# Two projections of a mixing block, moved in 512 columns of half the depth instead of 256 columns of the whole depth

## The chip, the cores and the metric

The kernel runs on one core of a Trainium2 chip. The metric is the device time of one execution in microseconds (us). A core has a matrix engine (TensorE, PE in the profile), a vector engine (VectorE, DVE), an activation engine (ScalarE, ACT), GpSimd (POOL) and SyncE (SP), which here issues the weight transfers. Matrix products are made in 128x128 steps: a stationary tile is loaded, a moving tile of up to 512 columns streams past it, and the sum stands in one of eight PSUM banks, 512 float32 columns wide.

## The reference

A first block of two layers works on x (512 tokens, width 1024, float32); each layer has a gated feed-forward part, a mix part and a second feed-forward part. A second block follows, which the change doesn't touch. The mix part is this:

```python
u = rmsnorm(x, g_mix[l])
p = u @ w_in[l]                       # width 3712: Fourier 1024, dilated 3 x 384, differential q, k, v 3 x 512
a_in = p[..., :c0]                    # Fourier
qc, kc, vc = p[..., c3:c4], p[..., c4:c5], p[..., c5:]
y_a = fourier_mix(a_in) @ w_br_a[l]   # real part of a 2-D DFT over tokens and the 128 channels of each of 8 groups
y_b = dilated_mixture(qb, kb, vb, rel_bias[:, :DIL_HEADS]) @ w_br_b[l]
y_c = diff_attention(qc, kc, vc, ...) @ w_br_c[l]
gates = jax.nn.sigmoid(u @ w_gate[l] + b_gate[l]).reshape(Bsz, S, N_BRANCHES, D)
merged = gates[:, :, 0] * y_a + gates[:, :, 1] * y_b + gates[:, :, 2] * y_c
x = x + merged @ w_out[l]
```

The two projections that change are `a_in` (1024 columns) and `vc` (512 columns), each 512 tokens by 1024 deep.

## The kernel before

x is held transposed, as 8 tiles of 128 channels x 512 tokens. Every float32 operand is split into a high part and a low part (`hi`, `lo`), and `mm3` (lines 196 to 199) makes each product of three matmuls: high x high (L197), high x low (L198), low x high (L199). Two kinds of projection are made so. `form_a` leaves the result transposed: the weights are stationary and 512 tokens move. `form_b` leaves tokens in the partitions: 128 tokens of x are stationary and the weights move. `form_b_pair` (L503) runs `form_b` for two token tiles into the two halves of one PSUM bank, 256 weight columns each, and evicts each half with ACT.

`weights` (L98) brings a chunk of weights, usually 128 x 8 x 256 (8 depth tiles of 256 columns): one DMA issued by SyncE into `raw` (tag `wr`), then two pieces, each a copy by ACT into `wh` (L108) and a subtraction by DVE into `wl` (L109). The tags `wr`, `wh` and `wl` have two buffers each, so two split chunks can exist, and a third one's split waits until every matmul of the first has run. Work tiles of 128 x 512 have the tag `g`, of which there are 32.

`mix` writes the work of a layer in one order: the dilated and differential q and k projections, the values projection (two chunks of 256 columns, between steps of the dilated attention), the differential attention interleaved with the gates of branches 1 and 2 (18 rounds; rounds 16 and 17 hold `project(0)` and `project(1)`), then the Fourier branch interleaved with its gates. The Fourier branch has four chunks of 256 columns, two groups each. `project(c)` makes the projection, adds and subtracts the token halves and splits these into parts; `sequence(c)` transforms over the tokens from the parts; `channels(c)` transforms over the channels and leaves tiles for the last merge.

The framework (Tile) derives all waits and orders each engine's queue with a planner: it takes the first written instruction that is ready by its own reckoning of time. So an engine's queue can leave the written order, and is fixed before the program runs; on the chip each engine takes its queue in that order.

Of the kernel before, what the change touches and what calls it, by code (L numbers as in the profile page):

```python
# [17 lines left out]
P = 128  # L18
# [32 lines left out]
class Kern:  # L51
# [45 lines left out]
    def weights(self, src, k0=0, nk=None):  # L97

        nc = self.nc
        src = src[:, k0:k0 + nk, :] if nk is not None else src  # L100
        _, nk, n = src.shape
        raw = self.wp.tile([P, nk, n], F32, tag="wr", name=self.nm("wr"), bufs=2)
        nc.sync.dma_start(raw, src)
        hi = self.wp.tile([P, nk, n], F32R, tag="wh", name=self.nm("wh"))
        lo = self.wp.tile([P, nk, n], F32R, tag="wl", name=self.nm("wl"))
        for j in range(0, n, P):
            js = slice(j, j + P)
            nc.scalar.activation(hi[:, :, js], raw[:, :, js], AF.Copy)  # L108
            nc.vector.tensor_tensor(out=lo[:, :, js], in0=raw[:, :, js], in1=hi.bitcast(F32)[:, :, js],  # L109
                                    op=ALU.subtract)  # L110
        return hi, lo
# [119 lines left out]
    def form_b(self, out, w, t, xs, start=True):  # L231

        ts = slice(t * P, (t + 1) * P)
        for k, x in enumerate(xs):
            self.mm3(out, (x[0][:, ts], x[1][:, ts]), (w[0][:, k, :], w[1][:, k, :]), start and k == 0,
                     k == len(xs) - 1)


    def tt(self, out, a, b, op, eng=None):
# [453 lines left out]
    def fourier_steps(self, l, xs, rcol, ya):  # L693
        st = {}

        def project(c):
            w = self.weights(self.ins["w_in_a"][l][c])
            a = [self.g(), self.g()]
            for t in range(0, 4, 2):
                self.form_b_pair(w, t, xs, rcol, lambda i: a[t // 2][:, i * 256:(i + 1) * 256])  # L700
            parts = []
            for op in (ALU.add, ALU.subtract):
                s = self.g()
                self.tt(s, a[0], a[1], op)
                parts.append(self.split(s))
            st[c] = parts

        def sequence(c):
            sh, sl = self.ft_seq
            parts, out = st[c], []  # L710
            for gi in range(2):
                pe, po = self.bank(), self.bank()
                for par, b in ((0, pe), (1, po)):
                    for k in range(2):
                        cs = slice(k * 256 + gi * P, k * 256 + gi * P + P)
                        at = slice(par * 256, par * 256 + 256)
                        self.mm3(b[:, 0:256], (parts[par][0][:, cs], parts[par][1][:, cs]),
                                 (sh[k][:, at], sl[k][:, at]), k == 0, k == 1)

                hi, lo = self.g(F32R), self.g(F32R)  # L720
                for b, at, ds in ((pe, 0, slice(0, 129)), (po, 0, slice(129, 385)), (pe, 129, slice(385, 512))):
                    src = b[:, at:at + ds.stop - ds.start]
                    self.split(src, hi[:, ds], lo[:, ds])
                out.append((hi, lo))
            st[c] = out

        def channels(c):
            ch, cl = self.ft_ch
            for hi, lo in st[c]:
                bu, bv = self.bank(), self.bank()  # L730
                for b, at, n, cs in ((bu, 0, 258, slice(0, P)), (bv, 256, 256, slice(P, 2 * P))):
                    self.mm3(b[:, 0:n], (ch[:, cs], cl[:, cs]), (hi[:, at:at + n], lo[:, at:at + n]), True, True)
                u, y = self.g(), self.g()
                self.act(u[:, 0:257], bu[:, 0:257], AF.Copy)
                self.act(y[:, 0:257:256], bu[:, 0:129:128], AF.Copy)
                ve, vo = bv[:, 129:256], bv[:, 1:129]
                self.tt(y[:, 2:256:2], u[:, 1:128], ve, ALU.subtract)
                self.tt(y[:, 1:256:2], u[:, 129:257], vo, ALU.subtract)
                self.tt(y[:, 510:256:-2], u[:, 1:128], ve, ALU.add)
                self.tt(y[:, 511:256:-2], u[:, 129:257], vo, ALU.add)  # L740
                ya.append(self.split(y))

        return project, sequence, channels


    def mix(self, l):
# [8 lines left out]
        def chunk(key, src):  # L755
            if key not in held:
                held.clear()
                held[key] = self.weights(src)
            return held[key]

        def dil(n):
            w = chunk(("d", n // 2), w_in[6 + n // 2] if n < 8 else ins["w_in_vb"][l])
            return self.form_a(w, n % 2, xs)

        def diff(n):
# [5 lines left out]
        def gate(i, n):  # L771
            w = chunk(("g", i, n // 2), ins["w_gate"][l][i * 4 + n // 2])
            b = self.form_a(w, n % 2, xs)
            t = self.side(n) if i == 1 else self.g()
            self.tt(t, b, R, ALU.mult)
            at = l * 24 + i * 8 + n
            self.act(t, t, AF.Tanh, scale=0.5, bias=self.bh[:, at:at + 1])
            th[i, n] = t
# [45 lines left out]
        for i in range(9):  # L824
            if i < 8:
                scores(*todo[i])
            if i > 0:
                turn(*todo[i - 1])
            if i < 7:
                diff(i + 1)  # L830
            elif i == 7:
                v = [t[:, at:at + S] for t in (self.big(), self.big()) for at in (0, S)]
                w = chunk(("v", 0), w_in[4])
                self.form_b_pair(w, 0, xs, rcol, lambda i: v[i][:, 0:256])
            else:
                self.form_b_pair(w, 2, xs, rcol, lambda i: v[2 + i][:, 0:256])
            if i > 0:
                values(*todo[i - 1])
            if i == 6:
                qk[0] = self.stacked(cT[4], cT[0])  # L840
        w = chunk(("v", 1), w_in[5])
        self.form_b_pair(w, 0, xs, rcol, lambda i: v[i][:, 256:512])
        fin()
        branch_b()
        self.form_b_pair(w, 2, xs, rcol, lambda i: v[2 + i][:, 256:512])
        scores, turn, values, finish = self.diff_steps(l, qk, v, yc)
        todo = [(h, qb) for h in range(4) for qb in range(4)]
        project, sequence, channels = self.fourier_steps(l, xs, rcol, ya)
# [28 lines left out]
        channels(0)  # L877
        project(2)
        sequence(1)
        gate(0, 2)  # L880
        channels(1)
        project(3)
        sequence(2)
        gate(0, 3)
        channels(2)
# [904 lines left out]
def layout(inputs):  # L1790
    f = {k: np.asarray(v) for k, v in inputs.items()}
    d = {"x": np.ascontiguousarray(f["x"][0].T.reshape(KD, P, S))}
    p = []
    for name, n in PARAMS:
        v = f[name]
        if name in ("s5_lambda_re_2", "s5_lambda_im_2"):
            v = v[0].reshape(16, P)
        elif name == "s5_log_dt_2":
            v = np.repeat(v[0], 64).reshape(16, P)
        p.append(_cols(v))  # L1800
    d["params"] = np.ascontiguousarray(np.concatenate(p, axis=1))
    for name in ("w_ffn1_gate", "w_ffn1_up", "w_ffn1_down", "w_ffn2_gate", "w_ffn2_up", "w_ffn2_down", "w_gate",
                 "w_br_a", "w_br_c", "w_out"):
        d[name] = _chunks(f[name])
    d["w_br_b"] = _chunks(f["w_br_b"], 512)
    w = f["w_in"]
    d["w_in_a"] = _chunks(w[:, :, 0:1024])
    order = np.concatenate([w[:, :, 2688:3200], w[:, :, 2176:2688], w[:, :, 3200:3712], w[:, :, 1024:2048]], axis=2)
    d["w_in"] = _chunks(order)
    d["w_in_vb"] = _chunks(w[:, :, 2048:2176], P)[:, 0]  # L1810
    d["rel_bias"] = f["rel_bias"]
    lam = np.stack([f["lam_q1"], f["lam_k1"], f["lam_q2"], f["lam_k2"]], axis=1)
    d["lam_v"] = lam.reshape(1, 512)
    d["even_w_in"] = _chunks(f["even_w_in_2"][0])
    d["even_w_out"] = _chunks(f["even_w_out_2"][0])
    d["s5_w_glu"] = _chunks(f["s5_w_glu_2"][0])
    w = f["odd_w_in_2"][0]
    d["odd_w_in"] = _chunks(w[:, 0:3072])
    d["odd_w_r"] = _chunks(w[:, 3072:3088], 16)[0]
    d["odd_w_out"] = _chunks(f["odd_w_out_2"][0])  # L1820
    d["gla_w_gate"] = f["gla_w_gate_2"][0]
    for n in ("s5_b_re", "s5_b_im"):
        b = f[n + "_2"][0].reshape(16, P, 16)
        d[n] = np.ascontiguousarray(b.transpose(1, 0, 2).reshape(P, 256))
    for n in ("s5_c_re", "s5_c_im"):
        c = f[n + "_2"][0].transpose(0, 2, 1).reshape(16, P, 16)
        d[n] = np.ascontiguousarray(c.transpose(1, 0, 2).reshape(P, 256))
    d.update(_consts())
    return d
# [16 lines left out]
```

## Time and profile before

| | |
|---|---|
| median of three executions | 3039.03 us (3038.86 to 3041.94) |
| profiled execution | 3038.39 us |
| its span, first to last instruction | 3036.7 us |
| PE busy | 3015.5 us, 99% |
| weight loads of PE | 2645.0 us, 87% |
| DVE busy | 2037.7 us, 67% |
| ACT busy | 1352.4 us, 45% |
| granted clock of PE | 1.00 |

The profile is of one execution; its times count from the first instruction, and the span is a little shorter than the time of the execution. A busy share is a mean over all stages. Matmuls are pipelined: the durations shown overlap, and a matmul's place in the stream is read from its start. The mix part of the first layer runs from about 339 to 830 us, that of the second from about 1533 to 2030 us. A row of the timeline has the start, the duration, engine, line, operation, tiles (out<-in by the program's names) and shape; in brackets stands the idle time of the engine before it and what ended it.

### The profile page before, as it was taken

Reading aid. Unit: us, or ns where it says so; the run is one execution under the profiler, and the core shown is the slowest. Engines: PE = TensorE matmul, PEld = TensorE weight load, DVE = VectorE, ACT = ScalarE, POOL = GpSimd, SP = SyncE. Lnnn points to the kernel's source line nnn. Section 1 sums busy time; section 2 is a strip of 40 time slices with the busy share of each in tenths; the row PEclk is TensorE's granted clock in tenths of the full one; section 3 lists DMA queues with packets and bytes.
Section 4 is the critical chain, followed back from the end, with each engine's and each line's share of the span. In section 5 each row is a group of like instructions: output and inputs, shape, how many; then the busy total and the mean of one; then the engine's idle time right before and its main releaser. Section 6 shows DMA issues by size and latency. Waiting matters only on the chain.

```text
span 3036.7 us, 44149 instructions
## 1 busy us (share of the span) xinstructions
PE 3015.5 (99%) x17718; PEld 2645.0 (87%) x17718; DVE 2037.7 (67%) x3646; ACT 1352.4 (45%) x2380; POOL 177.8 (6%) x310
## 2 busy tenths in 40 slices
PE   9999999999999999999999999999999999999999
PEld 7898889889889988889988889888999898877887
DVE  7798745646567979878874565557788855554633
ACT  5343435544343435433433554444334456663532
POOL 1001000000000011001120000000000011110010
PEclk9999999999999999999999999999999999999999
DMA  4232333322222333223343432222232332312221
GB/s 153 105 103 105 118 108 115 111 78 98 92 90 98 114 121 121 98 98 110 107 140 108 122 108 91 75 97 91 104 112 89 124 131 100 108 53 84 95 70 56
DMA packets 73358, 311.14 MB, mean 102 GB/s; under 512 B 18836, under 2 KB 20564, under 8 KB 44608
## 3 DMA queue, kind: packets, MB, share of 16 engines
q1 hardware_dynamic: 59680, 282.39, 27.0%
q10 hardware_dynamic: 9296, 16.47, 1.9%
q0 software_dynamic: 4176, 9.46, 1.2%
q8 instruction: 139, 2.28, 0.3%
q14 instruction: 67, 0.55, 0.1%
HBM read 292.47 MB, written 12.66 MB: 100 GB/s over the span
## 4 chain that ended last, share of the span: by engine, by line
PE 94%; ACT 2%; issue 1%; DVE 1%; DMA 1%; POOL 0%; SPq 0%; POOLq 0%; ACTq 0%; DVEq 0%
PE b L197 29%; PE b L199 29%; PE b L198 29%; PE b L202 7%; PE b L266 2%; ACT g L250 1%; ACT L250 0%; ACT sb L250 0%; DMA g<-tb 0%; DVE wl L109 0%; POOL sb L1259 0%; POOL y L240 0%; DVE g L240 0%; DMA g<-s_kst 0%; DMA wr<-in_w_ffn_gate 0%
## 5 line engine op out<-in xcount | busy, mean ns | idle before, releaser
L197 PE MATMUL b<-xh,wh 128*128 128x512 f32 (+1 forms) x1880 | 692.6, 368 | 7.3 <-ACT xh L250 6.8
L198 PE MATMUL b<-xl,wh 128*128 128x512 f32 (+1 forms) x1880 | 682.4, 363 | 1.1 <-DVE xl L94 1.1
L199 PE MATMUL b<-xh,wl 128*128 128x512 f32 (+1 forms) x1880 | 682.8, 363 | 0.5 <-DVE wl L94 0.5
L108 ACT ACTIVATE wh<-wr 128x1024 fp32r<-128x1024 f32 (+2 forms) x396 | 383.2, 1005 | 537.2 <-PE b L198 350.3
L109 DVE TENSOR_TENSOR wl<-wr,wh 128x1024 fp32r<-128x1024 f32 (+2 forms) x396 | 453.2, 1162 | 137.0 <-ACT wh L108 135.4
L197 PE MATMUL b<-g,wh 128*128 128x512 f32 x1168 | 456.6, 391 | 0.5 <-ACT g L93 0.5
L199 PE MATMUL b<-g,wl 128*128 128x512 f32 x1168 | 454.8, 389 | 1.2 <-DVE wl L109 1.2
L198 PE MATMUL b<-g,wh 128*128 128x512 f32 x1168 | 454.8, 389 | 0.2 <-DVE g L94 0.2
L197 PEld LDWEIGHTS b<-xh,wh 128*128 128x128 f32 x1880 | 355.7, 189 | 62.4 <-ACT xh L250 6.8
L198 PEld LDWEIGHTS b<-xl,wh 128*128 128x128 f32 x1880 | 355.8, 189 | 57.3 <-issue 2.2
L199 PEld LDWEIGHTS b<-xh,wl 128*128 128x128 f32 x1880 | 355.2, 189 | 57.8 <-DVE wl L94 0.9
L240 DVE TENSOR_TENSOR g<-b,g 128x512 f32<-128x512 f32 (+2 forms) x265 | 184.2, 699 | 235.3 <-PE b L199 220.8
L199 PEld LDWEIGHTS b<-g,wl 128*128 128x128 f32 x1168 | 219.2, 188 | 47.9 <-DVE wl L109 2.0
L197 PEld LDWEIGHTS b<-g,wh 128*128 128x128 f32 x1168 | 219.3, 188 | 47.5 <-issue 2.0
L198 PEld LDWEIGHTS b<-g,wh 128*128 128x128 f32 x1168 | 219.3, 188 | 45.3 <-DVE g L94 0.5
L197 PE MATMUL b<-wh,xh 128*128 128x256 f32 x896 | 256.9, 287 | 0.0
L198 PE MATMUL b<-wl,xh 128*128 128x256 f32 x896 | 254.5, 284 | 1.0 <-DVE wl L109 1.0
L199 PE MATMUL b<-wh,xl 128*128 128x256 f32 x896 | 253.6, 283 | 0.0
L240 DVE TENSOR_TENSOR g<-g,g 128x512 f32<-128x512 f32 (+8 forms) x371 | 200.8, 570 | 66.7 <-ACT g L250 62.3
L240 DVE TENSOR_TENSOR g<-g,b 128x256 f32<-128x256 f32 (+1 forms) x484 | 176.9, 397 | 31.2 <-PE b L199 27.3
L93 ACT ACTIVATE sw<-s 128x512 fp32r<-128x512 f32 x180 | 111.8, 630 | 193.3 <-DVE s L240 159.2
L250 ACT ACTIVATE g<-g 128x512 f32<-128x512 f32 (+4 forms) x280 | 143.6, 528 | 96.5 <-DVE g L240 88.3
(242 smaller groups left out, 5117.2 us busy)
## 6 DMA issues: line engine op xcount, KB each, us to landing
wr<-in_w_ffn_up SPq DMA_DIRECT2D x44, 1024.0 KB, 4.8
wr<-in_w_ffn_gate SPq DMA_DIRECT2D x43, 1024.0 KB, 4.8
wr<-in_w_ffn_down SPq DMA_DIRECT2D x32, 1024.0 KB, 4.8
wr<-in_w_gate SPq DMA_DIRECT2D x24, 1024.0 KB, 4.8
wr<-in_w_in SPq DMA_DIRECT2D x20, 1024.0 KB, 4.8
wr<-in_even_w_in SPq DMA_DIRECT2D x20, 1024.0 KB, 5.1
wr<-in_w_ffn_down SPq DMA_DIRECT2D x16, 768.0 KB, 4.3
g<-tb ACTq DMA_DIRECT2D x48, 256.0 KB, 3.1
```

The source lines that it names most:

```text
L93: self.nc.scalar.activation(hi, src, AF.Copy)
L108: nc.scalar.activation(hi[:, :, js], raw[:, :, js], AF.Copy)
L109: nc.vector.tensor_tensor(out=lo[:, :, js], in0=raw[:, :, js], in1=hi.bitcast(F32)[:, :, js], op=ALU.subtract)
L197: t.matmul(out, l[0], r[0], start=start, stop=False)
L198: t.matmul(out, l[0], r[1], start=False, stop=False)
L199: t.matmul(out, l[1], r[0], start=False, stop=stop)
L202: self.nc.tensor.matmul(out, l, r, start=start, stop=stop)
L240: return (eng or self.nc.vector).tensor_tensor(out=out, in0=a, in1=b, op=op)
L250: self.nc.scalar.activation(out, a, f, **kw)
L266: self.nc.tensor.transpose(out, a, self.ident)
```

## The change

Weights of the Fourier and the values projection are laid out on the host in chunks of 512 columns instead of 256 (the values get an array of their own, `w_in_v`, and the index of the dilated chunks moves by two). A new function `broad` loads such a chunk as two halves of the depth, 128 x 4 x 512 each, which have the size of a chunk before. It gives two steps. The first makes token tiles 0 and 1, one after the other, each over both halves; the second makes tiles 2 and 3, both over the first half and then both over the second. A tile fills a whole PSUM bank and is evicted by one ACT instruction of 512 columns. Two old chunks of Fourier are one pair now: `project(c)` with even c is the first step, with odd c the second, and the sums, differences and parts of both chunks are made after the second. The values projection's steps stand where its first chunk's two pairs stood, and its second chunk's two pairs, which stood around `fin()` and `branch_b()`, are gone. In the written order `gate(0, 2)` moves from before `channels(1)` and `project(3)` to behind them, and `channels(1)` to behind `project(3)`.

```diff
@@ weights
-        for j in range(0, n, P):
-            js = slice(j, j + P)
+        step = P if n < S else 256
+        for j in range(0, n, step):
+            js = slice(j, j + step)
             nc.scalar.activation(hi[:, :, js], raw[:, :, js], AF.Copy)
...
+    def broad(self, src, xs, rcol, out):
+        h = KD // 2
+        w = []
+        def step(second):
+            if not w:
+                w.extend([self.weights(src, 0, h), self.weights(src, h, h)])
+            ts = [2, 3] if second else [0, 1]
+            b = {t: self.bank() for t in ts}
+            order = [(t, i) for i in range(2) for t in ts] if second else [(t, i) for t in ts for i in range(2)]
+            for t, i in order:
+                cs = slice(t * P, (t + 1) * P)
+                for k in range(h):
+                    x = xs[i * h + k]
+                    self.mm3(b[t], (x[0][:, cs], x[1][:, cs]), (w[i][0][:, k, :], w[i][1][:, k, :]), i + k == 0,
+                             i == 1 and k == h - 1)
+                if i == 1:
+                    self.act(out(t), b[t], AF.Copy, scale=rcol[:, t:t + 1])
+        return lambda: step(False), lambda: step(True)
...
@@ fourier_steps
         def project(c):
-            w = self.weights(self.ins["w_in_a"][l][c])
-            a = [self.g(), self.g()]
-            for t in range(0, 4, 2):
-                self.form_b_pair(w, t, xs, rcol, lambda i: a[t // 2][:, i * 256:(i + 1) * 256])
-            parts = []
+            if c % 2 == 0:
+                a = st["a"] = [self.g() for _ in range(4)]
+                st["steps"] = self.broad(self.ins["w_in_a"][l][c // 2], xs, rcol, lambda t: a[t])
+                st["steps"][0]()
+                return
+            st["steps"][1]()
+            a, parts = st["a"], []
             for op in (ALU.add, ALU.subtract):
-                s = self.g()
-                self.tt(s, a[0], a[1], op)
-                parts.append(self.split(s))
-            st[c] = parts
+                parts.append([])
+                for t in range(2):
+                    s = self.g()
+                    self.tt(s, a[t], a[t + 2], op)
+                    parts[-1].append(self.split(s))
+            st[c - 1] = st[c] = parts
...
@@ mix
             elif i == 7:
                 v = [t[:, at:at + S] for t in (self.big(), self.big()) for at in (0, S)]
-                w = chunk(("v", 0), w_in[4])
-                self.form_b_pair(w, 0, xs, rcol, lambda i: v[i][:, 0:256])
+                v_steps = self.broad(ins["w_in_v"][l], xs, rcol, lambda t: v[t])
+                v_steps[0]()
             else:
-                self.form_b_pair(w, 2, xs, rcol, lambda i: v[2 + i][:, 0:256])
+                v_steps[1]()
...
-        w = chunk(("v", 1), w_in[5])
-        self.form_b_pair(w, 0, xs, rcol, lambda i: v[i][:, 256:512])
         fin()
         branch_b()
-        self.form_b_pair(w, 2, xs, rcol, lambda i: v[2 + i][:, 256:512])
...
         channels(0)
         project(2)
         sequence(1)
+        project(3)
+        channels(1)
         gate(0, 2)
-        channels(1)
-        project(3)
         sequence(2)
```

## Rows read from the trace of the kernel before

**Rows 1.** The page, part 1: busy us, share of the span, instructions.
```profile
PE 3015.5 (99%) x17718; PEld 2645.0 (87%) x17718; DVE 2037.7 (67%) x3646; ACT 1352.4 (45%) x2380; POOL 177.8 (6%) x310
```
**Rows 2.** The page, part 4: the chain that ended last, by engine.
```profile
PE 94%; ACT 2%; issue 1%; DVE 1%; DMA 1%; POOL 0%; SPq 0%; POOLq 0%; ACTq 0%; DVEq 0%
```
**Rows 3.** Windows of the mix stages: length, busy PE, PEld, DVE, ACT, POOL; clock.
```profile
339.00:830.00 491.00, 490.58 (x2704) 426.16 (x2704) 278.75 (x531) 217.65 (x431) 11.23 (x13) 1.00 0.31 104
1533.00:2030.00 497.00, 496.46 (x2746) 430.69 (x2745) 288.41 (x547) 220.98 (x438) 21.36 (x29) 1.00 0.32 106
```
**Rows 4.** Timeline of PE in project(0): start us, duration, line, operation.
```profile
632.08 0.28 PE L199 MATMUL b<-wh,xl 128*128 128x256 f32 x1
...
632.44 0.28 PE L199 MATMUL b<-wh,xl 128*128 128x256 f32 x1
```
**Rows 5.** Timeline of PE in the merge of branch 2.
```profile
671.36 0.39 PE L197 MATMUL b<-g,wh 128*128 128x512 f32 x1
...
672.04 0.39 PE L197 MATMUL b<-g,wh 128*128 128x512 f32 x1
```
**Rows 6.** PE windows in turn: project(0), merge 2, channels(0), gate(0,0), half a values chunk.
```profile
631.75:643.33 11.58, 11.58 (x99) 1.00 0.32 104
...
671.35:693.10 21.75, 21.75 (x97) 1.00 0.37 125
693.11:694.55 1.44, 1.44 (x13) 1.00 0.90 336
...
659.95:665.42 5.47, 5.47 (x26) 1.00 0.31 96
476.09:481.92 5.83, 5.83 (x51) 1.00 0.78 225
```
**Rows 7.** Timeline of ACT behind project(0): two 256-column evictions, one of 512.
```profile
643.55 0.84 ACT L250 ACTIVATE g<-b,y 128x256 f32<-128x256 f32 x2 [4.92 <-PE b L199]
...
648.72 0.59 ACT L250 ACTIVATE g<-b 128x512 f32<-128x512 f32 x1
```
**Rows 8.** DMA issues: transfers, count, KB each, median us to landing.
```profile
wr<-in_w_in_a SPq DMA_DIRECT2D x8, 1024.0 KB, 4.8
```
**Rows 9.** Timeline of DVE, second piece of the second values chunk.
```profile
476.57 1.23 DVE L109 TENSOR_TENSOR wl<-wr,wh 128x1024 fp32r<-128x1024 f32 x1 [0.20 <-ACT wh L108]
```
**Rows 10.** Timeline of ACT, both pieces of project(1)'s chunk.
```profile
630.49 1.06 ACT L108 ACTIVATE wh<-wr 128x1024 fp32r<-128x1024 f32 x1 [1.18 <-PE b L198]
...
633.82 1.04 ACT L108 ACTIVATE wh<-wr 128x1024 fp32r<-128x1024 f32 x1
```
**Rows 11.** Timeline of DVE, second piece of the same chunk.
```profile
634.90 1.23 DVE L109 TENSOR_TENSOR wl<-wr,wh 128x1024 fp32r<-128x1024 f32 x1 [0.70 <-ACT wh L108]
```
**Rows 12.** Timeline of DVE, second piece of the chunk split behind merge 2.
```profile
697.96 1.22 DVE L109 TENSOR_TENSOR wl<-wr,wh 128x1024 fp32r<-128x1024 f32 x1
```
**Rows 13.** Timeline of PE behind project(1): the values matmuls of the last round.
```profile
656.20 1.06 PE L202 MATMUL b<-sb,g 128*128 128x128 f32 x8
```
**Rows 14.** Timeline of DVE behind project(0): first sum, last part.
```profile
644.42 0.69 DVE L240 TENSOR_TENSOR g<-g,g 128x512 f32<-128x512 f32 x1 [6.76 <-ACT g L250]
...
648.85 0.68 DVE L94 TENSOR_TENSOR g<-g,g 128x512 fp32r<-128x512 f32 x1
```
**Rows 15.** Timeline of ACT, first piece of project(0)'s chunk.
```profile
613.92 1.06 ACT L108 ACTIVATE wh<-wr 128x1024 fp32r<-128x1024 f32 x1 [0.31 <-PE b L198]
```
**Rows 16.** Timeline of PE in the second block: transposes (L266), a projection (L197).
```profile
2561.04 0.48 PE L266 MATMUL b<-cc,g 128*128 128x128 f32 x2 [1.43 <-DVE g L244]
2561.28 0.37 PE L197 MATMUL b<-wh,xh 128*128 128x256 f32 x1
2561.48 0.29 PE L266 MATMUL b<-cc,g 128*128 128x128 f32 x1
```
**Rows 17.** Timeline of PE in the second block: second matmul of a projection.
```profile
2858.22 0.39 PE L198 MATMUL b<-wl,xh 128*128 128x256 f32 x1 [1.05 <-DVE wl L109]
```
**Rows 18.** Timeline of PE in round 15: the transposes ahead of a gate.
```profile
624.52 0.66 PE L266 MATMUL b<-cc,g 128*128 128x128 f32 x4 [0.42 <-DVE y L499]
```

More of the change, by code (lines that the diff above doesn't have):

```diff
@@ L714, in sequence @@
                     for k in range(2):
-                        cs = slice(k * 256 + gi * P, k * 256 + gi * P + P)
+                        cs = slice((c % 2) * 256 + gi * P, (c % 2) * 256 + gi * P + P)
                         at = slice(par * 256, par * 256 + 256)
-                        self.mm3(b[:, 0:256], (parts[par][0][:, cs], parts[par][1][:, cs]),
+                        self.mm3(b[:, 0:256], (parts[par][k][0][:, cs], parts[par][k][1][:, cs]),
                                  (sh[k][:, at], sl[k][:, at]), k == 0, k == 1)
@@ L761, in dil @@
         def dil(n):
-            w = chunk(("d", n // 2), w_in[6 + n // 2] if n < 8 else ins["w_in_vb"][l])
+            w = chunk(("d", n // 2), w_in[4 + n // 2] if n < 8 else ins["w_in_vb"][l])
             return self.form_a(w, n % 2, xs)
@@ L1806, in layout @@
     w = f["w_in"]
-    d["w_in_a"] = _chunks(w[:, :, 0:1024])
-    order = np.concatenate([w[:, :, 2688:3200], w[:, :, 2176:2688], w[:, :, 3200:3712], w[:, :, 1024:2048]], axis=2)
+    d["w_in_a"] = _chunks(w[:, :, 0:1024], 512)
+    d["w_in_v"] = _chunks(w[:, :, 3200:3712], 512)[:, 0]
+    order = np.concatenate([w[:, :, 2688:3200], w[:, :, 2176:2688], w[:, :, 1024:2048]], axis=2)
     d["w_in"] = _chunks(order)
```

## The prediction

> **What bounds the kernel now.** I read the page's first part, then its chain, then the windows by stage, then the timelines. The page has TensorE (PE) busy for 3015.5 of 3036.7 us; VectorE (DVE) stands at 67% and ScalarE (ACT) at 45% [rows 1]. The chain that ended last is PE for 94% of its length, and no other engine has over 2% [rows 2]. The change lies in the two mix stages. There PE is idle for 0.42 us of 491 and 0.54 us of 497, at a granted clock of 1.00, which is the 2.4 GHz level [rows 3]. So there is no wait to win back: only fewer or cheaper matmuls can shorten the stage, and every new PE wait is paid in full. DVE has 43% of these stages free and ACT 56% [rows 3], enough for moved work, if it comes in time.
>
> **Change 1: the matmuls.** A projection (Fourier or values) multiplies 4 token tiles by 8 depth tiles in 3 terms, 96 matmuls for 256 output columns. Per layer there are 4 such chunks for Fourier and 2 for values: 576 matmuls of 256 columns, 1152 in both layers. Afterwards half as many, 576, move 512 columns each; products and weight bytes are the same. PE's busy time can't price this, since a matmul shown with 0.28 us starts 0.12 us after the one before; starts must be read. Three steps of 256 columns take 0.36 us [rows 4], three of 512 take 0.68 us [rows 5]: 0.120 and 0.227 us each, so two halves cost 0.013 us more than one whole. Whole stretches (their counts also hold matmuls that end in them) say the same: 96 matmuls of 256 take 11.58 us and 48 take 5.83, while 96 of 512 take 21.75 [rows 6]. Before: per layer 4 x 11.58 + 4 x 5.83 = 69.6 us, for two layers 139.3. After: 3 pairs of chunks per layer at 21.75, six in all, 130.5. The saving is 8.8 us by stretches and 1152 x 0.120 - 576 x 0.227 = 7.5 by starts. The stretches of 256 columns begin behind transposes and hold the slow start of a step, which the stretch of 512 doesn't, so I take 7.8, near the lower.
>
> The Trainium skill ("TensorE: Matmul & The Clock Gate", Back-to-back issue gap) speaks against the change: it gives columns / 2.4 plus only some 2.5 ns, so 109.2 and 215.8 ns, and the sum would be 1.4 us saved. This trace has 120 and 227 ns, so the measurement decides.
>
> **Change 2: evictions, adds, splits.** Four 512-column evictions replace eight of 256 per pair of chunks. Two of 256 take 0.84 us together, one of 512 takes 0.59 [rows 7]; ACT saves about 1 us per pair, hidden, as ACT is not the bound. Adds, subtractions and part splits keep their number and shape (four 512-wide adds, four splits per pair). The pieces of the weight split keep 1024 elements (4 x 256 instead of 8 x 128). Each half is 1024 KB in 8 KB lines as before, 4.8 us to landing [rows 8], issued by SyncE as soon as one of two raw buffers is free. Cost on the path: none, while PE has other work.
>
> **Change 3: both weight buffers are held at once.** This is the risk. A pair needs both halves, and there are two buffers. The second half can be split only when the preceding step's last matmul has let its buffer go, and PE wants it after 12 matmuls of the first half, 2.7 us, its low part 0.2 us later. Before, the same buffer's chunk had a whole 11.6 us chunk of PE work ahead of it, so the pieces' times in the trace can be taken over.
> - Values: the low part's last piece ends at 476.57 + 1.23 = 477.8 [rows 9]; the projection starts at 476.1 [rows 6], and the need is 479.0. No wait; 1.2 us to spare.
> - First Fourier pair: the projection starts at 631.76 [rows 6]; the need of the low part is 634.7. ACT's second piece runs at 633.82, behind exponentials [rows 10], DVE's ends at 634.90 + 1.23 = 636.1 [rows 11]: 1.4 us late.
> - Second Fourier pair: start 694.55 (the channels stretch before it ends there [rows 6]), need 697.5; DVE's second piece ends at 697.96 + 1.22 = 699.2, behind the subtractions of the channel step [rows 12]: 1.7 us late.
> Nothing behind PE's waiting matmul would run, and ACT's first 512-column eviction would wait with it. The cover would be the second token tile's 12 matmuls on the first half (2.7 us, another PSUM bank), if the planner that orders each engine's queue puts them ahead.
>
> Behind the pair the release goes well: the second step runs the first half for both tiles first, so its buffer is free 24 matmuls (5.4 us) before the step ends. The slow split above took 5.6 us from release to low part (630.49 to 636.1), and at least the 1.06 us of values matmuls [rows 13] lie between the step and the next use.
>
> **Change 4: the sums wait for all four tiles.** Sums and differences used to be ready one chunk before their sequence step. Now both chunks' parts exist only after tile 3. From a projection's end (643.33) to the last part (648.85 + 0.68 = 649.5) the trace has 6.2 us [rows 6, 14], with two pieces of a weight split in between. After the first pair, the written order has only the values matmuls (1.06 us [rows 13]) ahead of the sequence step: 5.1 us to wait. If the planner takes the gate projection first (5.47 us [rows 6]), 6.5 us cover 6.2. After the second pair the new written order puts the channel step and that gate projection in between, 1.44 + 5.47 = 6.9 us [rows 6]: covered. That is what moving the gate past the fourth projection and the channel step does; its weight transfer also moves behind both Fourier halves in SyncE's queue, but has over 20 us until it is used.
>
> **Does the planner pull ahead?** The first Fourier chunk's split ran on ACT at 613.92 [rows 15], 18 us before its use and ahead of softmax work that is written first: yes on ACT. On PE, transposes written ahead of a projection are interleaved with its matmuls at 2561 [rows 16]: yes, too. But there PE first stood idle for 1.43 us, and once a projection waited 1.05 us for the low part of its weights [rows 17]; before a gate PE waited 0.42 us for a transpose written ahead of it [rows 18]. So it covers, and misjudges by about 1 us. Per layer the places A, B (late halves) and C (parts) cost between 0 and 1.4 + 1.7 + 5.1 = 8.2 us. I take one miss like those two rows (1.05 and 1.43) in two layers, and none at the other five places: 1.4 us.
>
> **Sum.** 3038.39 (the profiled execution, 1.7 us of it outside its span) - 7.8 + 1.4 = 3032.0. The median shown is 0.6 us higher, and from it the sum is 3032.6; I predict 3032.3. A change of 0.2%, 6.1 us, is about what a measurement of this kernel can tell from none. The bound, 3032.95, lies right above the forecast.
>
> **Rivals.**
> 1. Late halves (A and B): the queue keeps the written order inside the first steps and PE waits 3.1 us per layer. For it: the 1.05 us row [rows 17]. Against it: 12 ready matmuls in another bank. Time 3038.7 - 7.8 + 6.2 = 3037.1 (3038.7 is the middle of profile and median): no change that can be told. Chance 0.18.
> 2. The other side: PE keeps the written order throughout, above all in front of the sequence step. The place is C, where the parts come 5.1 us too late; with A and B as results of the same order it is 8.2 us per layer. Time 3038.7 - 7.8 + 16.4 = 3047.3, slower. It decides from 7 us per layer on. For it: PE kept to the written order where it waited in the mix stage [rows 18]. Against it: the interleaved transposes [rows 16]. Chance 0.07.
> 3. The saving does not exist: the stream of columns alone sets the spacing, two halves cost one whole, and the new waits remain: 3038.7 + 1.4 = 3040.1. Both ways of reading the spacing are against it [rows 4 to 6], by 0.013 us or more per pair. The Trainium skill's page that is named above would leave 1.4 us of the saving. Chance 0.05.
> 4. Room: the eight part tiles now live until the sequence step of the pair's second chunk, across eight merges. By the code I count 32 tiles of tag g alive around the last gate before the merges (8 gate tiles, 8 of the attention output, 8 parts, 4 of the sequence output, 2 Fourier gates, the row scale, the channel matrix), and there are 32. A write would then wait for a release, about one token tile of 2.9 us per layer (half of the 5.83 that two tiles take [rows 6]): 3032.3 + 5.8 = 3038.1. Chance 0.06.
>
> **Chances.** The forecast (new waits of at most 3.5 us, so 3030.9 to 3034.4) gets 0.64, the rivals 0.36. Inside it nearly four fifths lie below the bound: waits can't be under zero, and to pass it they must exceed 2.05 us, a full miss in both layers. So faster has 0.5. Slower is rival 2 with a hundredth from rival 3, 0.08, and the same has the remaining 0.42. The range starts at 3030.0 (no new wait, and the saving of 8.8) and ends at 3038.5, which takes in rivals 1 and 4.
>
> **What would show it.** Right: 1152 fewer 256-column and 576 more 512-column matmuls on PE, 0.227 us apart; an idle PE of 1 to 3 us in both mix windows together; in front of the first pair's sequence step the gate's matmuls. Wrong: idle of PE charged to the low split of the weights at the 13th matmul of a pair (rival 1), to ACT or DVE part splits in front of the sequence step (rival 2), or to tiles that come free late (rival 4); 512-column starts further apart than 0.227 us would break the main term.

## The result and the profile after

The changed kernel takes 3065.93 us (median of 4 executions, 3065.62 to 3066.31). The kernel before took 3040.20 beside it (4 executions, 3038.86 to 3041.94). The ratio is 1.0084, with a 95% interval of 1.0067 to 1.0102: slower by 0.8%, or 25.7 us, where 3032.3 and a range of 3030.0 to 3038.5 had been forecast. The forecast was wrong in sign and size. In its sum the new waits stood at 1.4 us; they cost 32.4.

First the page of the changed kernel: its busy times, and the head of the chain that ended last.

```profile
span 3064.0 us, 42986 instructions
...
PE 3024.3 (99%) x17142; PEld 2624.7 (86%) x17142; DVE 2039.9 (67%) x3646; ACT 1350.1 (44%) x2356; POOL 178.4 (6%) x310
...
PE 93%; DVE 2%; ACT 2%; issue 1%; DMA 1%; POOL 0%; SPq 0%; ACTq 0%; POOLq 0%; DVEq 0%
```

PE's share hardly moves against [rows 1, 2], though 25 us have been added. The windows of the two mix stages say where to look (columns as in [rows 3]).

```profile
339.00:830.00 491.00, 481.63 (x2360) 405.03 (x2359) 272.20 (x521) 211.00 (x411) 12.27 (x13) 0.99 0.31 101
1533.00:2030.00 497.00, 487.41 (x2406) 409.63 (x2405) 284.14 (x544) 215.20 (x421) 21.23 (x29) 0.99 0.31 103
```

PE is now idle for 9.4 and 9.6 us there, where it was idle for 0.42 and 0.54 [rows 3], and the clock is 0.99 instead of 1.00. The view of PE's waits, for the first mix stage, splits the idle by what PE waited for (total, times, longest):

```profile
PE b L290 <- DVE g L271: 5.4, 1, 5.4
PE b L198 <- ACT g L93: 2.7, 4, 0.9
PE b L200 <- DVE g L94: 0.5, 2, 0.3
PE b L290 <- DVE y L523: 0.5, 1, 0.5
```

The last row was there before, as 0.4 (line numbers differ a little from kernel to kernel). The first is new: the transposes (L290) of the differential attention's first unit (one head, one block of queries) wait for its softmax product (L271). Rows two and three are place C, the first pair's sequence step waiting for ACT's and DVE's splits of the sums (0.2 us of them belong to the second pair's). No row names the low split of the weights (L110): the late halves at A, at B and in the values cost nothing.

Both new waits cost more than their idle time. Here are PE's timeline at the first one (start, duration, idle before it in brackets) and the windows around it.

```profile
515.27 1.07 PE L203 MATMUL b<-g,g 128*128 128x512 f32 x4
521.71 1.11 PE L290 MATMUL b<-cc,g 128*128 128x128 f32 x4 [5.37 <-DVE g L271]
522.47 0.78 PE L198 MATMUL b<-xh,wh 128*128 128x512 f32 x1
523.05 0.63 PE L199 MATMUL b<-xl,wh 128*128 128x512 f32 x1
523.47 0.63 PE L200 MATMUL b<-xh,wl 128*128 128x512 f32 x1
...
527.26 0.39 PE L198 MATMUL b<-xh,wh 128*128 128x512 f32 x1
527.48 0.39 PE L199 MATMUL b<-xl,wh 128*128 128x512 f32 x1
```

```profile
510.00:515.00 5.00, 5.00 (x23) 4.14 (x23) 1.24 (x2) 1.02 (x2) 0.00 (x0) 1.00 0.19 53
515.00:520.00 5.00, 1.33 (x6) 0.76 (x5) 5.00 (x12) 4.95 (x10) 0.00 (x0) 0.98 0.51 108
520.00:525.00 5.00, 3.29 (x10) 2.81 (x11) 4.45 (x11) 1.42 (x3) 0.00 (x0) 0.50 0.95 296
525.00:530.00 5.00, 5.00 (x19) 3.99 (x19) 2.37 (x9) 3.05 (x9) 0.00 (x0) 0.83 0.05 16
```

Behind the idle time the granted clock is 0.50, the 1.2 GHz level, and 512-column matmuls start 0.43 us apart instead of 0.227 [rows 5]. The last two rows are 0.22 us apart again. Adding up what each interval between starts has over the usual one for its width gives 5.5 us for the wait and 2.4 us for the thirteen slow starts behind it: 7.9 us. The same sum at the sequence step (662.8 to 673.6) gives 7.0 us. Of these 3.1 are idle; 2.5 are slow starts behind the last wait, at the half clock; and 1.4 lie between the five pieces of the wait, mostly at a clock of 1.00, where a matmul behind a wait and the one after it start later than the idle time shown says.

```profile
660.00:665.00 5.00, 3.77 (x21) 2.97 (x19) 2.47 (x5) 2.45 (x5) 0.00 (x0) 1.00 0.35 105
665.00:670.00 5.00, 3.16 (x13) 2.50 (x13) 3.51 (x6) 1.81 (x4) 0.00 (x0) 0.66 0.29 105
```

The second pair's sequence step (739.8 to 743.4) adds 1.3 us, with 0.4 of idle and the clock at 1.00 throughout. Per layer 16.2 us are added (16.0 by the same sums in the second layer), and 3.5 are saved by the matmuls: 12.7 us, 25.4 in two layers, against 25.7 measured.

The matmuls themselves did what was forecast. By shape, those that move weight columns in the changed kernel (count, then busy time and mean ns):

```profile
L198 PE MATMUL b<-wh,xh 128*128 128x256 f32 x512 | 147.3, 288 | 0.0
...
L198 PE MATMUL b<-wh,xh 128*128 128x512 f32 x192 | 74.8, 393 | 0.0
```

Times three terms (L198 to L200) that is 576 of 512 columns. Summed from start to start they take 132.0 us; the 1152 of 256 columns that they replace took 139.0. The saving is 7.0 us.

### The profile page after: what moved, and what is told of

It reads as the page before. It is cut to its first block, busy times and chain, and to the rows that moved or that the text cites. A ratio compares the mean times of both kernels' runs of the same rounds, so it can differ in the third digit from the quotient of the medians.

```text
span 3064.0 us, 42986 instructions
## 1 busy us (share of the span) xinstructions
PE 3024.3 (99%) x17142; PEld 2624.7 (86%) x17142; DVE 2039.9 (67%) x3646; ACT 1350.1 (44%) x2356; POOL 178.4 (6%) x310
## 4 chain that ended last, share of the span: by engine, by line
PE 93%; DVE 2%; ACT 2%; issue 1%; DMA 1%; POOL 0%; SPq 0%; ACTq 0%; POOLq 0%; DVEq 0%
PE b L198 28%; PE b L200 28%; PE b L199 28%; PE b L203 7%; PE b L290 2%; DVE wl L110 1%; ACT sb L274 1%; ACT g L274 1%; ACT L274 0%; DVE g L264 0%; DMA g<-tb 0%; DVE g L94 0%; ACT wh L109 0%; ACT g L93 0%; POOL y L264 0%
## 5 line engine op out<-in xcount | busy, mean ns | idle before, releaser
L198 PE MATMUL b<-xh,wh 128*128 128x512 f32 (+1 forms) x1880 | 695.2, 370 | 8.1 <-ACT xh L274 7.3
L200 PE MATMUL b<-xh,wl 128*128 128x512 f32 (+1 forms) x1880 | 684.6, 364 | 0.5 <-DVE wl L94 0.5
L110 DVE TENSOR_TENSOR wl<-wr,wh 128x1024 fp32r<-128x1024 f32 (+2 forms) x396 | 453.3, 1162 | 187.8 <-ACT wh L109 186.1
L198 PE MATMUL b<-g,wh 128*128 128x512 f32 x1168 | 457.1, 391 | 0.5 <-ACT g L93 0.5
L200 PE MATMUL b<-g,wl 128*128 128x512 f32 x1168 | 455.6, 390 | 1.2 <-DVE wl L110 1.2
L198 PEld LDWEIGHTS b<-xh,wh 128*128 128x128 f32 x1880 | 357.2, 190 | 63.7 <-ACT xh L274 7.3
L200 PEld LDWEIGHTS b<-xh,wl 128*128 128x128 f32 x1880 | 356.4, 190 | 58.0 <-DVE wl L94 0.9
L264 DVE TENSOR_TENSOR g<-b,g 128x512 f32<-128x512 f32 (+2 forms) x265 | 184.4, 701 | 227.8 <-PE b L200 221.0
L200 PEld LDWEIGHTS b<-g,wl 128*128 128x128 f32 x1168 | 219.6, 188 | 47.9 <-DVE wl L110 2.0
L198 PEld LDWEIGHTS b<-g,wh 128*128 128x128 f32 x1168 | 219.7, 188 | 47.6 <-issue 2.0
L198 PE MATMUL b<-wh,xh 128*128 128x256 f32 (+1 forms) x704 | 222.1, 316 | 0.0
L199 PE MATMUL b<-wl,xh 128*128 128x256 f32 (+1 forms) x704 | 221.0, 314 | 1.1 <-DVE wl L110 1.1
L200 PE MATMUL b<-wh,xl 128*128 128x256 f32 (+1 forms) x704 | 219.9, 312 | 0.0
L264 DVE TENSOR_TENSOR g<-g,g 128x512 f32<-128x512 f32 (+8 forms) x371 | 201.6, 574 | 6.7 <-ACT g L274 2.3
L264 DVE TENSOR_TENSOR g<-g,b 128x256 f32<-128x256 f32 (+1 forms) x484 | 177.7, 400 | 30.7 <-PE b L200 26.9
```

Source lines behind the costliest of these rows:

```text
L198: t.matmul(out, l[0], r[0], start=start, stop=False)
L199: t.matmul(out, l[0], r[1], start=False, stop=False)
L200: t.matmul(out, l[1], r[0], start=False, stop=stop)
L264: return (eng or self.nc.vector).tensor_tensor(out=out, in0=a, in1=b, op=op)
```

## The experiments

Each ran beside the kernel before on the same chip (its medians there are 3040.95 to 3041.49; single executions of it lie between 3038.3 and 3043.5). Gains are against the changed kernel's 3065.93, whose kernel before had 3040.20, so they are good to some 1.5 us. Theory at the start: the loss is two new waits with the half clock behind them, one from each part of the change. Rival: one wait with consequences.

**Each part alone.** The first kernel takes `project`, `sequence` and the order of the Fourier steps from before; the second takes the values from before:

```
-                v_steps = self.broad(ins["w_in_v"][l], xs, rcol, lambda t: v[t])
-                v_steps[0]()
+                w = chunk(("v", 0), ins["w_in_v"][l][0])
+                self.form_b_pair(w, 0, xs, rcol, lambda i: v[i][:, 0:256])
...
+        w = chunk(("v", 1), ins["w_in_v"][l][1])
+        self.form_b_pair(w, 0, xs, rcol, lambda i: v[i][:, 256:512])
         fin()
         branch_b()
+        self.form_b_pair(w, 2, xs, rcol, lambda i: v[2 + i][:, 256:512])
```

> Only the values projection moves 512 columns of half the depth; the Fourier part is as before. Theory (each part of the change carries its own new wait, and the 512-column stream still saves a third of its 7.0 us here): minus 2.3 us for the stream, plus 2 x 7.9 us at the first transposes of the differential attention (5.5 us of idle and 2.4 us of matmuls at half clock behind it, per layer): 3040.2 - 2.3 + 15.8 = 3053.7. Rival (the wait at the transposes comes out of the Fourier part's transfers or tiles): 3037.9.

> Only the Fourier projection moves 512 columns of half the depth; the values are as before. Theory: minus 4.7 us for the stream, plus 2 x (7.0 + 1.3) us in front of the sequence steps, and no new wait at the differential attention's first transposes: 3040.2 - 4.7 + 16.6 = 3052.1. Rival (the wait at the sequence step is a late consequence of the values' wait): 3035.5.

Measured: values alone 3052.14 us (ratio 1.0038, 1.0023 to 1.0053), Fourier alone 3052.23 (1.0038, 1.0024 to 1.0053). They add 11.2 and 11.3 us; together the change adds 25.7. Some 1.7 of the missing 3.2 us lie in the clock: with Fourier alone the same sequence step costs 5.9 and 6.2 us in the two layers instead of 7.0 and 6.8. The rest is within the scatter of single executions. The waits of PE in the first mix stage are cleanly parted: with the values alone only the transposes wait, with Fourier alone only the sequence step does.

```profile
PE b L291 <- DVE g L272: 5.3, 1, 5.3
PE b L291 <- DVE y L524: 0.6, 1, 0.6
```

```profile
PE b L198 <- ACT g L93: 2.9, 4, 0.9
PE b L290 <- DVE y L523: 0.5, 1, 0.5
PE b L200 <- DVE g L94: 0.5, 2, 0.3
```

**Why the transposes wait.** The chain in the changed kernel, read back from 521.71 through the timelines of DVE, ACT, ACT's DMA queue and SyncE's:

```profile
504.38 0.33 SPq L103 DMA_DIRECT2D wr<-in_w_gate  x1
504.75 0.42 SPq L820 DMA_DIRECT2D g<-in_w_br_b  x1
...
511.32 0.63 ACT L93 ACTIVATE g<-g 128x512 fp32r<-128x512 f32 x1 [1.43 <-DMA g<-in_w_br_b]
511.40 0.33 ACTq L485 DMA_DIRECT2D g<-tb  x1
...
514.46 0.69 DVE L523 CUSTOM_DVE_ANT_0 g<-b,g 128x512 f32<-128x512 f32 x1 [1.78 <-DMA g<-tb]
...
517.55 1.21 DVE L110 TENSOR_TENSOR wl<-wr,wh 128x1024 fp32r<-128x1024 f32 x1
...
518.76 1.20 DVE L110 TENSOR_TENSOR wl<-wr,wh 128x1024 fp32r<-128x1024 f32 x1
...
520.90 0.75 DVE L271 SCALAR_TENSOR_TENSOR g<-g,y,g 128x512 f32<-128x512 f32 x1
```

The second load of branch b's weights stands on SyncE's queue behind a gate chunk that waits for a raw buffer, and goes out at 504.75. ACT's split of it waits, and the bias transfer for the first softmax, which ACT issues, stands behind that split. Before the change both loads were issued together:

```profile
494.81 0.33 SPq L103 DMA_DIRECT2D wr<-in_w_gate  x1
495.20 1.66 SPq L792 DMA_DIRECT2D g<-in_w_br_b  x2
```

Two readings were open. Either the transfer is late, or the two values steps that used to stand around `fin()` and `branch_b()` were cover without which the chain is too long. Three kernels told them apart. The first moves the whole of `branch_b()`:

```
         fin()
-        branch_b()
...
             if i < 16:
                 scores(*todo[i])
+            if i == 0:
+                branch_b()
```

> The changed kernel, with the loads and splits of branch b's weights written behind the first scores of the differential attention, so that the bias transfer on ACT's queue no longer stands behind a split that waits for those weights. Theory (the queue, not the chain's own length): the wait at the first transposes goes, with the slow matmuls behind it, 2 x 7.9 = 15.8 us: 3065.9 - 15.8 = 3050.1. Rival (the softmax chain is simply too long for the 11 us of values work that no longer stands ahead of it): over half of the wait stays, 3058 or more.

Measured 3062.86 us (1.0073, 1.0058 to 1.0088): only 3.1 us gained, a miss. The first transposes no longer wait, but one step later the attention's product with the values does:

```profile
PE b L203 <- ACT g L274: 4.2, 1, 4.2
PE b L198 <- ACT g L93: 2.9, 4, 0.9
```

The splits of branch b now stand among the second unit's softmax work, and its bias goes out at 515.63; the eviction of the first transposes stands behind that unit's exponentials on ACT (526.66). The wait moved on. This run seemed to speak for lost cover. The second kernel puts half of the cover back, by cutting the values' second step by depth:

```
-                v_steps[1]()
+                v_steps[2](0)
...
         fin()
         branch_b()
+        v_steps[2](1)
```

`v_steps[2](i)` is a new function of `broad` that runs tiles 2 and 3 over half i of the depth (24 matmuls) and evicts them after the second.

> The changed kernel, with the second step of the values cut by depth: its first 24 matmuls stay where the step is, its other 24 are written behind the loads and splits of branch b's weights, so that 5.45 us of PE work stand there again. Theory (lost cover: the two values steps that stood around the end of the dilated attention hid the whole chain of weights, bias transfer and first softmaxes): the idle at the first transposes and its half-clock matmuls go and come back nowhere: 3065.9 - 2 x 7.9 = 3050.1. Rival (half of the old cover is too little; a wait of some us moves on, as it did in the run before): 3058 or more.

Measured 3049.88 us (1.0030, 1.0018 to 1.0042): 16.1 us gained, as expected, and no wait at the transposes. But this edit also lets the chain start earlier, so it can't say which of the two it cured. The third moves no PE work at all and only issues the transfers earlier:

```
             elif i == 7:
+                raws = load_b()
...
-        branch_b()
+        branch_b(raws)
```

`load_b()` holds the two DMAs, `branch_b(raws)` the splits.

> The changed kernel, with only the two transfers of branch b's weights issued earlier, ahead of the values' first step; their splits stay where they are, and no PE work is moved. In the changed kernel the second of them stands on SyncE's queue behind a gate chunk that waits for a raw buffer, and goes out at 504.75 instead of 495 to 497. Theory (this late transfer, and the bias transfer and softmax that queue behind its split on ACT, is what the lost values steps uncovered): the bias goes out near 502, the idle at the first transposes goes with its half-clock matmuls: 3065.9 - 15.8 = 3050.1. Rival (without the PE work that stood there the chain is too long even with its weights in time): over half of the wait stays here or behind, 3058 or more.

Measured 3048.72 us (1.0024, 1.0015 to 1.0034): 17.2 us gained. The timelines of ACT's queue, DVE and PE show the bias out at 502.73 and the last product of the unit at 513.15, before PE comes to the transposes at 515.71:

```profile
502.73 0.33 ACTq L485 DMA_DIRECT2D g<-tb  x1
503.39 1.18 ACT L93 ACTIVATE g<-g 128x512 fp32r<-128x512 f32 x2
...
508.58 0.68 DVE L523 CUSTOM_DVE_ANT_0 g<-b,g 128x512 f32<-128x512 f32 x1
...
513.15 0.75 DVE L271 SCALAR_TENSOR_TENSOR g<-g,y,g 128x512 f32<-128x512 f32 x1
...
515.71 0.60 PE L290 MATMUL b<-cc,g 128*128 128x128 f32 x4
```

So the lost cover alone costs nothing here: with its weights in time the chain fits in front of PE without the two steps. What costs is the late transfer. The run with half the cover fits this: in it the second load goes out at 500.30 and the bias at 505.37, 4 and 6 us earlier than in the changed kernel.

**Is the slow clock the price of the wait?** A kernel that puts useless matmuls where PE was idle:

```
+            if i == 2:
+                fb = self.bank()
+                for _ in range(24):
+                    self.mm(fb, xs[0][0][:, 0:P], xs[0][0])
             if i > 1:
                 turn(*todo[i - 2])
```

> The changed kernel with 24 more 512-column matmuls per layer (5.45 us), whose result nobody reads, in front of the first transposes of the differential attention, where PE stands idle for 5.4 us. They do no useful work; they only take the place of the idle. Theory (the matmuls at half clock behind it are the price of having been idle): 2 x 2.4 us less than the changed kernel although it does more, 3061.1, and granted clock 1.00 there. Rival (they are slow for a reason of their own, such as their operands or the transfers beside them): 3065.9 or above.

Measured 3062.70 us (1.0073, 1.0058 to 1.0088): 3.2 us faster than the changed kernel with 10.9 us more matmuls in it. The windows have full clock where the changed kernel has 0.50:

```profile
515.00:520.00 5.00, 5.00 (x24) 4.13 (x23) 4.33 (x8) 4.95 (x10) 0.00 (x0) 1.00 0.52 136
520.00:525.00 5.00, 5.00 (x25) 4.04 (x24) 4.54 (x12) 1.53 (x3) 0.00 (x0) 1.00 0.83 265
```

The expected 4.8 us weren't reached; a new wait of 1.34 us for ACT stands behind it in each layer (it ends at 529.96). With the same operands and the transfers still beside them (DMA share 0.83, 0.95 before) the matmuls run at full clock, so the slow ones come from the idle time. The Trainium skill ("TensorE: Matmul & The Clock Gate", HAM oscillation) says that waits between groups of matmuls throw the array back to the lower clock, so that each group pays again; these rows agree.

**Place C.** Two kernels try the two ways of curing it: the gate's matmuls first, or the sums in another order.

```
-        sequence(0)
         gate(0, 0)
+        sequence(0)
```

> The changed kernel, with the gate projection written ahead of the first sequence step instead of behind it. Theory (the sequence step waits for the parts of all four token tiles, 3.1 us of idle and 3.9 us of half clock per layer, and the 5.45 us of the gate are enough cover): 3065.9 - 2 x 7.0 = 3051.9. Rival (the parts are later than the gate covers, or the wait goes to what follows): 3060 or more.

```
-            for op in (ALU.add, ALU.subtract):
...
+            for t in range(2):
+                s = [self.g(), self.g()]
+                for i, op in enumerate((ALU.add, ALU.subtract)):
+                    self.tt(s[i], a[t], a[t + 2], op)
+                parts.append([self.split(s[i]) for i in range(2)])
```

> The changed kernel, with the sums and differences written by token tile: both sums of tiles 0 and 2, which only wait for tile 2, ahead of those of tiles 1 and 3, and each pair of sums ahead of its splits. Theory (half of the wait in front of the sequence step is the order sum, ACT split, DVE split, next sum, in which DVE waits 0.8 to 1.4 us for ACT four times): the last part comes 3 to 4 us earlier and idle plus half clock fall by 3 to 4 us per layer: 3059, between 3057 and 3061. Rival (the eviction of the fourth tile alone sets the wait): 3065 or more.

Gate first: 3055.64 us (1.0050, 1.0035 to 1.0065), 10.3 us gained of 14.0. The wait of 3.1 us falls to 0.4, but `finish(3)` (the transposes of the attention's last head), which now follows the sequence step directly, waits 0.8 us for ACT. Sums by tile: 3053.17 us (1.0042, 1.0027 to 1.0056), 12.8 us gained where 7 had been expected. DVE's timeline in the changed kernel shows why the order of the sums was worth so much: each sum (L264) stands behind the low split (L94) of the one before, which waits for ACT.

```profile
664.63 0.68 DVE L264 TENSOR_TENSOR g<-g,g 128x512 f32<-128x512 f32 x1
...
666.62 0.69 DVE L264 TENSOR_TENSOR g<-g,g 128x512 f32<-128x512 f32 x1
668.06 0.69 DVE L94 TENSOR_TENSOR g<-g,g 128x512 fp32r<-128x512 f32 x1 [0.76 <-ACT g L93]
668.67 0.69 DVE L264 TENSOR_TENSOR g<-g,g 128x512 f32<-128x512 f32 x1
670.11 0.69 DVE L94 TENSOR_TENSOR g<-g,g 128x512 fp32r<-128x512 f32 x1 [0.76 <-ACT g L93]
```

So a part comes every 2 us. Written by tile, two sums stand together (one row of two at 660.69 and one at 666.29), the sequence step's last wait ends at 665.2 instead of 668.1, and the wait at the second pair is gone as well. The clock stays at 1.00 there: the sequence step costs 1.9 us instead of 7.0.

**All together, and the main term by itself.** The cut values step, the gate first and the sums by tile in one kernel; and the same kernel with each 512-column matmul issued as two of 256:

```
+                    for n, js in enumerate((slice(0, 256), slice(256, 512))):
-                    self.mm3(b[t], (x[0][:, cs], x[1][:, cs]), (w[i][0][:, k, :], w[i][1][:, k, :]), i + k == 0,
+                        self.mm3(b[t][:, js], (x[0][:, cs], x[1][:, cs]), (w[i][0][:, k, js], w[i][1][:, k, js]),
```

> The changed kernel with three edits together: the values' second step cut by depth around the branch weights, the gate projection ahead of the first sequence step, the sums by token tile. Theory (the new waits at two places are all that the change cost, and they add): 3065.9 - 15.8 - 14.0 = 3036.1, below the kernel before. Rival (waits only move on): 3042 or more.

> The kernel with all three covers, but each 512-column matmul of the two projections issued as two of 256 columns, as many as before the change: buffers, steps and order stay. Theory (the saving is 0.013 us per pair of halves, some 7.0 us over 576 of them by the starts in the traces): 3034.1 + 7.0 = 3041.1, level with the kernel before. Rival (the saving lies in the evictions and staging, or isn't there): 3034 to 3036.

> The kernel with all three covers once more, beside the one with halves, since 0.2% is at stake. Theory: 6 to 8 us below the kernel before and 7 us below the one with halves. Rival: within 0.1% of either.

Measured: 3034.10 us (0.9977, 0.9967 to 0.9986), and again 3034.84 (0.9978, 0.9969 to 0.9987), faster than the kernel before. With halves 3041.38 (1.0000, 0.9991 to 1.0009), level with it. In the first mix stage of the combined kernel PE waits 0.6 us in all, and the clock is 1.00:

```profile
339.00:830.00 491.00, 490.39 (x2430) 413.84 (x2430) 282.40 (x534) 217.71 (x421) 11.32 (x13) 1.00 0.31 104
```

The second of these and the one with halves ran side by side; they differ by 6.5 us and in nothing but the width of 576 matmuls. That is the gain of the wider matmuls alone.

## Why the prediction was wrong, point by point

**The matmuls (change 1): right.** 7.8 us were taken, 7.5 by starts and 8.8 by stretches; the trace has 7.0 and the pair of kernels 6.5. The lower reading was the better one. Rival 3 falls by the pair of kernels. The Trainium skill ("TensorE: Matmul & The Clock Gate", Back-to-back issue gap) gives its formula, by which 1.4 us would be left, for an isolated matmul; it doesn't hold for this stream, in which each matmul loads its own weights (17142 loads for 17142 matmuls).

**Evictions, adds, splits (change 2): right.** None of them shows up as a wait.

**Late halves (change 3, A, B, values; rival 1): no cost.** PE doesn't wait for a low split in either mix stage. In the first Fourier pair, which starts at 638.68, the low part of the second half is ready only at 642.45 + 1.23 = 643.68, and by then PE has started 22 matmuls without a pause, where the written order would have asked for it at the 14th:

```profile
638.68 0.48 PE L198 MATMUL b<-wh,xh 128*128 128x512 f32 x1
...
643.57 0.62 PE L198 MATMUL b<-wh,xh 128*128 128x512 f32 x2
...
642.45 1.23 DVE L110 TENSOR_TENSOR wl<-wr,wh 128x1024 fp32r<-128x1024 f32 x1 [1.33 <-ACT wh L109]
```

So matmuls of the second tile were put ahead: the cover that was described, and the planner took it. A kernel without this order was not run.

**The step that failed first** is the cost of change 3 on queues, for the values: "No wait; 1.2 us to spare". The places that could cost anything in its sum were A, B and C in two layers; the transposes weren't among them. It asked when the moved steps need their weights, and not what else shifts when the second values chunk leaves its place. Its chunk and its two steps stood around `fin()` and `branch_b()`. With them gone the gate chunks' and branch b's transfers were queued in another order on SyncE, one load of 256 KB went out some 8 us later, and through ACT's queue (split, then bias transfer) it held up the first softmax: 5.4 us of idle per layer, 7.9 with what follows. The prediction weighed SyncE's queue for the moved Fourier gate, and didn't follow it for branch b. The run with early loads shows this as the cause: 17.2 us come back.

**The step that failed second** is place C. The price was right in kind: with the planner in the written order, "5.1 us to wait". The forecast let the planner take the gate first ("yes, too") and took "one miss like those two rows (1.05 and 1.43) in two layers". It kept the written order in both layers, and PE was idle for some 3.1 us in each, in five pieces. So half of rival 2 came true, without its parts A and B. The 6.2 us from the projection to the last part were read as a cost that can only be covered; the sums by tile show that much of it was the order of DVE's instructions.

**Left out: the clock and the restarts.** Every wait was priced at its idle time, against a stage that runs at 1.00 [rows 3]. Starts at half clock behind the two waits added 2.4 and 2.5 us per layer, 9.8 of the 32.4 us added in both; late starts between the pieces at C added another 1.4 per layer. (The expectation for the gate put all 3.9 down to the half clock.) With them the rival's 5.1 us at C would have been an estimated 9.0, and "it decides from 7 us per layer on" would have been met by C alone.

**The second pair's sequence step: nearly right.** It was called covered; it cost 1.3 us per layer, 0.4 of it idle. **Room (rival 4): no sign.** No wait for a tile's release is among PE's waits. **The base.** The forecast started from 3038.7; the kernel before took 3040.2 beside the changed one, which is 1.5 of the 33.6 us between forecast and measurement.

## What to carry to other kernels

When a step is taken out of its place, list what was queued beside it on every DMA-issuing engine and ask which transfer now stands behind one that waits for a buffer; the bill may come at a place that the diff doesn't touch. Price a PE wait at its idle time plus the late and half-clock starts behind it: in this kernel the whole came to 1.5 times the idle at one long wait and over twice at several short ones. And where sums and splits alternate between two engines, write the sums that are ready first together: the order alone was worth more here (12.8 us) than the change's own gain (6.5).

## What the runs showed of the hardware

Waits far shorter than 5 us can take the clock down too: at the sequence step the idle pieces are 0.92, 0.31, 0.88, 0.22 and 0.74 us, with matmuls between them, and the window 665 to 670 has clock 0.66. With the sums by tile only 0.92 and 0.30 us are left, and the clock stays at 1.00.

The fall isn't the same in each execution. Behind older waits late in the kernel (0.4, 0.5, 0.6 and 1.2 us in some 5 us) the profiled executions differ, though the waits are alike: in the kernel before the stretch has clock 1.00, in the changed one 0.66, and seven matmuls take 1.5 us longer.

```profile
2735.00:2740.00 5.00, 3.79 (x17) 2.79 (x16) 2.75 (x4) 1.28 (x1) 3.44 (x7) 1.00 0.25 55
```

```profile
2761.00:2766.00 5.00, 3.80 (x10) 2.70 (x9) 2.49 (x4) 1.27 (x1) 3.28 (x6) 0.66 0.27 76
```

That is most of the 1.9 us by which the two profiled spans (3064.0 and 3036.7) differ more than the 25.4 us worked out above. What decides it stays open. The scatter of the kernel before goes with the clock as well: beside the experiments the 14 executions of it with a mean granted clock of 1.000 took 3038.31 to 3039.46 us, the 37 with 0.999 took 3040.65 to 3043.45. The profile and the median that the forecast started from (3038.39 and 3039.03) lie in the first group.
